# Two more plain chunks in the first FFN, a second VectorE figure in the planner, and one high part at the heads of the second FFNs

## The chip, the cores and the metric

The kernel runs on one core of a Trainium2 chip. The metric is device time in microseconds (us) for one execution, which computes the whole network for one sequence of 256 tokens. A measurement is the median of several executions; beside it stands one execution taken with the hardware profiler, from which all durations of single instructions come.

The engines have short names in the profile: PE is TensorE's matmuls and PEld its weight loads, DVE is VectorE, ACT is ScalarE, POOL is GpSimd, SP issues the DMAs. Each engine works through its own queue in order.

## The reference

Two layers, all in float32, on x of 256 x 1024. The first layer mixes tokens with forgetting attention (FoX), the second with multi-head latent attention (MLA), whose compressed keys and values come from the stream between the layers.

```python
D_MODEL, SEQ, DEPTH, D_FF = 1024, 256, 2, 2816

def post_norm(x, delta, g, b):
    return layer_norm(ALPHA * x + delta, g, b)

def swiglu(x, w_in, w_out):
    h = x @ w_in
    gate, up = h[..., :D_FF], h[..., D_FF:]
    return (jax.nn.silu(gate) * up) @ w_out

for i in range(DEPTH):
    if i == N_A:
        k_nope, k_rope, v_shared = shared_kv(x, kv_w_down, kv_norm, kv_w_up, cos, sin)
    x = post_norm(x, 0.5 * swiglu(x, ffn1_w_in[i], ffn1_w_out[i]), ln_g[i, 0], ln_b[i, 0])
    mix = fox_mixer(...) if i < N_A else mla_mixer(...)
    x = post_norm(x, mix, ln_g[i, 1], ln_b[i, 1])
    x = post_norm(x, 0.5 * swiglu(x, ffn2_w_in[i], ffn2_w_out[i]), ln_g[i, 2], ln_b[i, 2])
    gate = jax.nn.sigmoid(x @ ple_w_gate[i] + ple_b_gate[i])
    x = post_norm(x, gate * (p[i] @ ple_w_proj[i]), ln_g[i, 3], ln_b[i, 3])
```

So there are four FFNs: two per layer, and each has gate and up weights of 1024 x 2816 and output weights of 2816 x 1024.

## The kernel before

**High and low parts.** Every product is made of three matmuls (`mm3`, L581). Each operand is held as a high part (a copy in the type `float32r`, made by ScalarE) and a low part (the operand less its high part, made by VectorE); high x high, high x low and low x high are added up. So each weight passes through ScalarE and VectorE before PE can use it. A *unit* is 128 x 1024 weights at most (`unit_of`, L404); two units share a raw buffer of one megabyte (a group, `group_of`, L387), and of raw buffers there are three. The next group is loaded on SP's queue when the buffer three groups back has been split (`split_done`, L308).

**The planner.** `Stream` (L145) decides, while the program is written, where among the matmuls each unit is split. It keeps clocks of its own for PE, ScalarE, VectorE and the DMAs (`pe_t`, `act_t`, `dve_t`, `dma_t`), which `busy` (L339) advances: a VectorE operation of n columns costs 150 + 1.05 n ns, a ScalarE one 200 + 0.84 n ns, a matmul 0.437 n + 4 ns. A split can be placed in four ways:

- `pump` (L357) is called after most products. It splits one unit if the unit's load should have arrived, a slot is free, and neither ScalarE nor VectorE is more than 1600 ns ahead of PE on these clocks. It does nothing while `hold` is set.
- `ahead` (L192) places only the high part and leaves the low part as `rest`; `later` (L208), or the next split, places the low part. While a `rest` is open, or no slot is free, or the load has not arrived, `ahead` returns without doing anything.
- `fill` (L199) splits up to a given number of units beyond the one in use.
- `use` (L369) splits at once what PE needs now and is not there yet.

There are ten slots `hl0` to `hl9`; others are lent and taken back (`lend`, `reclaim`).

**An FFN** (`ffn`, L697) cuts the 2816 hidden columns into 11 chunks of 256 (`NCH`). For each chunk, gate and up are computed: as `H` (L708), one half of the tokens at a time with x stationary, or as `HT` (L781), transposed, with the weights stationary and 256 tokens moving, 96 matmuls a chunk. The first FFN (`cold`) begins with `first` (L713) for chunk 0, while its weights still arrive, and has only transposed chunks after it; the others begin with H(0, 0), H(1, 0), H(0, 1), H(1, 1), in which the second number is the half of the tokens. In the middle of H(1, 0), after 12 of its matmuls (`HAT`), `other` transposes the other half of x.

The output product is made in one of two ways. *Summed* chunks use a scheme of seven products of blocks in place of eight: `add` (L814) makes sums of the chunk's activations and splits the 896 columns of forms, `Stream.add` (L267) makes sums of the weights (three VectorE operations), four units (`ws`) are split, and `sums` (L833) issues 21 matmuls of 128 x 512 per chunk. *Plain* chunks keep their activations as they are (512 columns, a tile of the ring `g4` of six), split two units (`wout`), and `W` (L904) issues 24 matmuls. The last three chunks (`STAG`) are always plain, and so are those in `early`. The order is: chunks up to 4, `sums` of those of them that are summed, chunks 5 to 7, their `sums`, `combine` (VectorE work that adds the seven products up), chunks 8 to 10, then `W` of the early chunks for both token halves, `W` of chunks 8 to 10 for the first half, the normalization `ln` of that half, `W` for the second half, and its `ln`.

**The mixers** (`fox`, L1089, and `mla`, L1467) run written lists, FOX and ORDER, after (FOX) or from (ORDER) their first projections. In the lists "f n" is `fill`, "a" is `ahead`, "l" is `later`, and "hold 1" and "hold 0" set and clear `hold`. The FOX list sets it from its key and query products on and clears it ahead of the last output products; ORDER begins with "hold 1" and clears it near its end. The per-layer embedding is `ple` (L1022).

`run` (L1786) calls, in order: the first FFN (`cold`), `fox`, the first layer's second FFN, `ple`, the second layer's first FFN (`kv`, which also makes the compressed keys and values), `mla`, the second layer's second FFN, `ple`.

Of the kernel before, what the change touches and what calls it, by code (L numbers as in the profile page):

```python
# [32 lines left out]
SW_H00 = 0  # L33
# [96 lines left out]
class Recorder:  # L130
    def __init__(self):
        self.seq = []
# [12 lines left out]
class Stream:  # L145


    def __init__(self, nc, raw_pool, pool, loads, seq):
        self.nc, self.raw_pool, self.pool, self.loads = nc, raw_pool, pool, loads
        seen = []  # L150
        self.groups = []
        for key in seq:
            g = group_of(key)
            if g not in seen:
                seen.append(g)
                self.groups.append(g)
        members = {g: [] for g in self.groups}
        self.left = {}
        for key in seq:
            if key not in self.left:  # L160
                self.left[key] = 0
                members[group_of(key)].append(key)
            self.left[key] += 1
        self.order = [k for g in self.groups for k in members[g]]
        self.index = {k: i for i, k in enumerate(self.order)}
        self.last_of = {members[g][-1]: i for i, g in enumerate(self.groups)}
        self.raw, self.hl, self.sums, self.added = {}, {}, {}, {}
        self.slots = [f"hl{i}" for i in range(NSLOT)]
        self.slot_of = {}
        self.kept = set()  # L170
        self.loaded = self.ready = 0
        self.done = 0
        self.pending = None
        self.pe_t = self.act_t = self.dve_t = self.dma_t = 0.0
        self.arrives = {}
        self.between = {}
        self.hold = False
        self.rest = None
        self.at = 0
        self.stop = None  # L180

    def load(self, n=NRAW):
        while self.loaded < len(self.groups) and self.loaded < self.done + n:
            g = self.groups[self.loaded]
            r = self.raw_pool.tile([128, 2048], F32, name="raw")
            self.loads(self.nc.sync, g, r, (1, 1, 2, 4)[min(self.loaded, 3)], self.between)
            self.raw[g] = r
            self.dma_t = max(self.dma_t, self.pe_t, self.dve_t) + DMA_NS * WIDTH.get(g[0], 2048) / 2048
            self.arrives[g] = self.dma_t + 2000
            self.loaded += 1  # L190
# [148 lines left out]
    def busy(self, act=0, dve=0, pe=0):  # L339

        if act:
            self.act_t = max(self.act_t, self.pe_t) + 200 + 0.84 * act
        if dve:
            self.dve_t = max(self.dve_t, self.pe_t) + 150 + 1.05 * dve
        if pe:
            self.pe_t += max(109, 0.437 * pe + 4)

# [39 lines left out]
def group_of(key):  # L387
    k = key[0]
    if k in ("win", "wiu", "fv", "kd", "dq"):
        return key[:-1] + (key[-1] // 2,)  # L390
    if k == "ws":
        return key[:-1]
    if k in ("wout", "fvb", "fvc", "fk", "fq", "fo", "pg", "pp", "mo", "qr"):
        return key[:-1] + (key[-1] // 2,)
    if k in ("kvk", "qn"):
        return ("kq", key[-1])
    return key
# [86 lines left out]
class Trunk:  # L484
# [212 lines left out]
    def ffn(self, li, which, lni, kv=False, ple=False, at=None, cold=False, after=()):  # L697


        nc, S = self.nc, self.S  # L700
# [1 line left out]
        g, gT, forms = {}, {}, {}  # L702
        homes = HOMES[:3] if kv else HOMES
        S.reclaim(*homes)
        early = (0,) if cold else (0, 1) if kv else (1,)
        summed = [c for c in range(NCH - STAG) if c not in early]

        def H(c, t, at=None, what=None, sweeps=0):  # L708
            ps = self.bank("h")
            self.moving(ps, t, ("win", li, which, c), 512, at, what, sweeps)  # L710
            act(c, t, ps)

        def first():  # L713

            ps = [self.bank("h") for _ in range(2)]
            key = lambda u: ("win", li, which, 0, u)

            def xs(k):
                def f():
                    self.parts(  # L720
                        self.xT[:, :, 0, k, :], self.xT[:, :, 1, k, :],
                        self.xraw[:, k, :].rearrange("p (t c) -> p t c", c=128),
                    )

                return f

            S.hold = True
            self.spare(self.bank("tr"))
            for u in range(4):
                if u == 0:  # L730
                    head = (("hi", 0, 0, 256), xs(0), ("lo", 0, 0, 256), ("both", 0, 256, 512))
                else:
                    head = (xs(2 * u), ("both", 0, 0, 512))
                S.split_pieces(key(u), head + (xs(2 * u + 1), ("both", 1, 0, 512)))
            for u in range(4):
                w = self.use(key(u))
                for kk in range(2):
                    k = 2 * u + kk
                    for i, j in ((0, 0), (1, 0), (0, 1)):
                        for b in range(4):  # L740
                            self.mm(
                                ps[b // 2][:, 256 * (b % 2) : 256 * (b % 2) + 256],
                                w[:, j, 512 * kk + 128 * b : 512 * kk + 128 * b + 128], self.xT[:, :, i, k, :],
                                (k, i, j, b % 2) == (0, 0, 0, 0), (k, j, b % 2) == (7, 1, 1),
                            )
                if u:
                    S.split()
            S.hold = False
            gt = self.room(0, summed)
            nc.scalar.activation(gt, ps[0], AF.Silu)  # L750
            close(0, gt, ps[1])

        def act(c, t, ps):
            if c not in g:
                g[c] = self.tl([128, 1024], F32, "P", 2) if c == 0 else self.tl([128, 512], F32, "g4", 6)
            gt = g[c][:, 256 * t : 256 * t + 256]
            nc.scalar.activation(gt, ps[:, 0:256], AF.Silu)  # L757
            nc.vector.tensor_tensor(gt, gt, ps[:, 256:512], op=ALU.mult)
            self.S.busy(act=256, dve=256)
# [144 lines left out]
        def W(c, ts, what=None):  # L904
            for kt in range(2):
                w = self.use(("wout", li, which, 2 * c + kt))
                for t in ts:
                    for n in range(2):
                        if kt == 1 and what:
                            what(n)  # L910
                        self.mm3(
                            z[t][n],
                            lambda i: gT[c][:, i, 256 * kt + 128 * t : 256 * kt + 128 * t + 128],
                            lambda i: w[:, i, 512 * n : 512 * n + 512],
                            (t, c, kt) == (0, early[0], 0), (c, kt) == (NCH - 1, 1),
                        )
# [4 lines left out]
        if cold:  # L921
            first()
        else:
            H(0, 0, sweeps=SW_H00)
            S.stop = ("wiu", li, which, 2, 0) if kv else None

            def other():
                self.XT(1)
                S.stop = None

            H(1, 0, HAT, other, SW_H10)
            if kv:
                self.kv_down(1)
            H(0, 1, sweeps=SW_H01)
            H(1, 1)
# [45 lines left out]
        for c in range(n - STAG, n):  # L981
            W(c, (1,), next_x if c == n - 1 else None)
        self.ln(1, z[1], 1.0, 4 * LN_EPS)

    def room(self, c, summed):
        self.full[c] = f = self.tl([128, 1024], F32, "P", 2)
        return f[:, 0:512]
# [912 lines left out]
```

## Time and profile before

| | |
|---|---|
| median of three runs | 1062.66 us |
| the three runs | 1059.51, 1062.89, 1062.66 us |
| the profiled execution, its time | 1060.52 us |
| its span, first to last instruction | 1058.7 us |
| its mean granted TensorE clock | 0.995 |
| HBM read | 200.55 MB, 190 GB/s over the span |

The span falls into these stages, by the first matmul of each (us from the start of the span, rounded): the first FFN from 0, `fox` from 193, the first layer's second FFN from 310, its embedding from 495, the second layer's first FFN from 519, `mla` from 705, the second layer's second FFN from 842, its embedding from 1026.

How to read the lines of the profile: a group or timeline line names the line of the kernel, the engine, the operation, the tiles written and read, shapes (partitions x elements) and count; a bracket in the timeline is the idle time of that engine just before, and what ended it. L589 is the one line by which all matmuls but transposes are issued, L241 and L242 are the high and low part of a weight split, L249 and L253 the same in the form that `ahead` places, L273, L279 and L281 the three weight sums, L803 the product of gate and up, L818, L822 and L823 the activations' sums, L606 a low part of activations. A matmul's tile names tell the stage: `y<-hl,fs` is a product of a split weight with a summed chunk's forms, which lie in `ota`, `otb`, `qk` or `fs`; `h<-xT,hl` is a gate or up product. Matmuls are pipelined, so the time per matmul is the distance from start to start.

### The profile page before, as it was taken

What the parts mean: (1) busy time and instruction counts of PE and PEld (TensorE: products, weight loads), DVE (VectorE), ACT (ScalarE), POOL (GpSimd) and SP (SyncE); (2) the same over time, 40 slices, a digit from 0 to 9 for tenths busy, and PEclk for the clock granted to TensorE, in tenths of its full rate; (3) what the DMA queues carried; (4) which work ended last, traced back from release to release, by engine and by line L of the source; (5) the groups of instructions that cost most, each with busy time, mean ns of one, the idle gap of its engine ahead of it and who ended that gap; (6) DMA issues with size and microseconds to landing.
All of it is one profiled execution on the core that took longest, in us unless ns stands there. A gap on an engine that the chain in (4) does not pass through costs nothing.

```text
span 1058.7 us, 17610 instructions
## 1 busy us (share of the span) xinstructions
PE 1037.5 (98%) x7091; PEld 949.4 (90%) x7091; DVE 883.9 (83%) x1296; ACT 587.0 (55%) x893; POOL 58.3 (6%) x88
## 2 busy tenths in 40 slices
PE   9999899999999999999999999999999999999996
PEld 8979799898878989998889999988999889899986
DVE  5897887868888889977978799778888889899776
ACT  6555465457846464663564646526776474655631
POOL 0000000113400000000040000000000000000000
PEclk9999999999999999999999999999999999999998
DMA  7846367446447465664575646642444465556522
GB/s 280 316 160 217 141 236 252 155 142 225 161 148 264 174 210 199 212 229 168 207 256 182 210 149 229 232 134 105 136 169 151 168 238 200 187 196 224 205 115 80
DMA packets 37477, 202.74 MB, mean 191 GB/s; under 512 B 3970, under 2 KB 9874, under 8 KB 16532
## 3 DMA queue, kind: packets, MB, share of 16 engines
q1 hardware_dynamic: 37396, 201.63, 53.6%
q8 instruction: 55, 0.90, 0.3%
q14 instruction: 26, 0.21, 0.1%
HBM read 200.55 MB, written 1.06 MB: 190 GB/s over the span
## 4 chain that ended last, share of the span: by engine, by line
PE 70%; ACT 2%; DVE 1%; issue 1%; DVEq 0%; ACTq 0%
PE h L589 37%; PE y L589 23%; PE tr L589 8%; PE tr L593 2%; PE h L593 0%; ACT P L1310 0%; ACT hl L241 0%; ACT qk L602 0%; ACT xT L1603 0%; DVE hl L242 0%; DVE x L681 0%; DVE tr L1685 0%; ACT L570 0%; ACT L757 0%; DVE y L1292 0%
## 5 line engine op out<-in xcount | busy, mean ns | idle before, releaser
L589 PE MATMUL h<-xT,hl 128*128 128x256 f32 x3408 | 394.8, 277 | 0.3 <-DVE hl L302 0.3
L589 PEld LDWEIGHTS h<-xT,hl 128*128 128x128 f32 x3408 | 391.8, 188 | 1.4 <-ACT xT L602 0.6
L242 DVE TENSOR_TENSOR hl<-raw,hl 128x1024 fp32r<-128x1024 f32 (+3 forms) x290 | 338.1, 1197 | 49.0 <-ACT hl L241 47.6
L241 ACT ACTIVATE hl<-raw 128x1024 fp32r<-128x1024 f32 (+3 forms) x290 | 287.7, 1031 | 77.3 <-DVE raw L281 21.9
L589 PE MATMUL y<-hl,g 128*128 128x512 f32 x396 | 92.5, 391 | 0.0
L589 PEld LDWEIGHTS y<-hl,g 128*128 128x128 f32 x396 | 73.7, 188 | 14.8
L589 PE MATMUL y<-hl,otb 128*128 128x512 f32 x264 | 69.3, 395 | 0.0
L589 PE MATMUL h<-hl,xT 128*128 128x512 f32 (+2 forms) x306 | 67.1, 371 | 1.4 <-ACT hl L241 1.4
L589 PEld LDWEIGHTS h<-hl,xT 128*128 128x128 f32 x306 | 53.4, 188 | 11.7 <-ACT hl L241 2.5
L589 PEld LDWEIGHTS y<-hl,otb 128*128 128x128 f32 x264 | 48.1, 188 | 9.5 <-DVE otb L606 0.3
L253 DVE TENSOR_TENSOR hl<-raw,hl 128x1024 fp32r<-128x1024 f32 (+2 forms) x42 | 50.0, 1195 | 2.2 <-ACT hl L249 2.1
L589 PE MATMUL y<-hl,ota 128*128 128x512 f32 x192 | 49.9, 393 | 0.0
L673 POOL TENSOR_TENSOR rs<-ve,mhalf 128x1 f32<-128x1 f32 x16 | 15.1, 943 | 623.5 <-DVE ve L672 623.5
L602 ACT ACTIVATE xT<-tr 128x512 fp32r<-128x512 f32 x28 | 16.1, 596 | 58.2 <-PE tr L593 58.2
L242 DVE TENSOR_TENSOR hl<-ts,hl 128x1024 fp32r<-128x1024 f32 (+1 forms) x52 | 48.0, 962 | 0.2 <-ACT hl L241 0.2
L249 ACT ACTIVATE hl<-raw 128x1024 fp32r<-128x1024 f32 (+2 forms) x42 | 43.1, 1029 | 7.1 <-DVE raw L281 6.1
L589 PE MATMUL tr<-xT,hl 128*128 128x256 f32 x384 | 45.3, 277 | 0.0
L589 PEld LDWEIGHTS tr<-xT,hl 128*128 128x128 f32 x384 | 44.5, 188 | 0.4
L589 PE MATMUL y<-hl,xT 128*128 128x512 f32 (+3 forms) x228 | 43.9, 340 | 0.0
L797 ACT ACTIVATE P<-h 128x512 f32<-128x512 f32 x33 | 19.6, 594 | 41.4 <-PE h L589 41.1
L241 ACT ACTIVATE hl<-ts 128x1024 fp32r<-128x1024 f32 (+1 forms) x52 | 41.9, 839 | 0.0
L589 PEld LDWEIGHTS y<-hl,ota 128*128 128x128 f32 x192 | 34.9, 188 | 6.6
(284 smaller groups left out, 1459.3 us busy)
## 6 DMA issues: line engine op xcount, KB each, us to landing
raw<-in_ffn_in_dram SPq DMA_DIRECT2D x85, 1024.0 KB, 4.9
raw<-in_ffn_out_dram SPq DMA_DIRECT2D x44, 1024.0 KB, 5.0
raw<-in_pg_dram SPq DMA_DIRECT2D x8, 1024.0 KB, 5.6
raw<-in_mo_dram SPq DMA_DIRECT2D x8, 1024.0 KB, 4.7
raw<-in_kq_dram SPq DMA_DIRECT2D x8, 640.0 KB, 4.5
gb<-in_ln_g_dram SPq DMA_DIRECT2D x8, 512.0 KB, 6.7
gb<-in_ln_b_dram SPq DMA_DIRECT2D x8, 512.0 KB, 6.3
raw<-in_fk_dram SPq DMA_DIRECT2D x4, 1024.0 KB, 4.9
```

The source lines that it names most:

```text
L241: nc.scalar.activation(hi, src, AF.Copy)
L242: nc.vector.tensor_tensor(lo, src, hi.bitcast(F32), op=ALU.subtract)
L249: nc.scalar.activation(hi, src, AF.Copy)
L253: nc.vector.tensor_tensor(lo, src, hi.bitcast(F32), op=ALU.subtract)
L589: self.nc.tensor.matmul(out, lhsT, rhs, start=start, stop=stop)
L593: self.nc.tensor.transpose(out, in_, self.ident)
L602: self.nc.scalar.activation(hi, src, AF.Copy)
L673: nc.gpsimd.tensor_tensor(rs, ve, self.mhalf, op=ALU.pow)
L797: nc.scalar.activation(gt, ps, AF.Silu)
```

## The change

Three edits, in `Stream` and `ffn`:

1. In the first FFN `early` is (0, 1, 2) where it was (0,). Chunks 1 and 2 become plain: five chunks (3 to 7) are summed where seven were, `sums` of the first group has two chunks where it had four, and `W` of three chunks stands behind chunk 10 where that of one stood. All 11 chunks' gate and up products stay as they are.
2. The constant 150 of a VectorE operation in `busy` becomes `self.fixed`. It is 150 inside an FFN and 80 elsewhere: in both mixers and in the embedding stages.
3. In the second FFN of each layer (neither `cold` nor `kv`), H(0, 0) calls `ahead` once after 12 of its 24 matmuls, as `moving` (L625) does it for `other` in H(1, 0).

```diff
@@ Stream.__init__
         self.stop = None
+        self.fixed = 80
@@ Stream.busy
         if dve:
-            self.dve_t = max(self.dve_t, self.pe_t) + 150 + 1.05 * dve
+            self.dve_t = max(self.dve_t, self.pe_t) + self.fixed + 1.05 * dve
@@ Trunk.ffn
         S.reclaim(*homes)
-        early = (0,) if cold else (0, 1) if kv else (1,)
+        S.fixed = 150
+        early = (0, 1, 2) if cold else (0, 1) if kv else (1,)
         summed = [c for c in range(NCH - STAG) if c not in early]
...
-            H(0, 0, sweeps=SW_H00)
+            H(0, 0, None if kv else 12, S.ahead, SW_H00)
             S.stop = ("wiu", li, which, 2, 0) if kv else None
...
         self.ln(1, z[1], 1.0, 4 * LN_EPS)
+        S.fixed = 80
```

## The prediction

> **What bounds the kernel now.** I read the busy row of the page first, then whom TensorE (PE) waited for (total, times, longest), then the two stretches in which most of it lies.
>
> ```profile
> PE 1037.5 (98%) x7091; PEld 949.4 (90%) x7091; DVE 883.9 (83%) x1296; ACT 587.0 (55%) x893; POOL 58.3 (6%) x88
> ```
>
> ```profile
> PE y L589 <- DVE hl L242: 4.6, 3, 2.1
> PE tr L589 <- DVE hl L242: 1.5, 2, 1.0
> PE h L589 <- ACT hl L241: 1.4, 2, 0.9
> ```
>
> PE is busy for 98% of the span, so a change can win by fewer matmuls or by closing the few holes. Apart from the start, the longest kinds of hole are waits for a weight's low part (VectorE, L242) and for a high part (ScalarE, L241). The first two kinds lie in the first FFN's two `sums` stages, which the first two rows below frame (columns: us; busy time and count of PE, weight loads, VectorE, ScalarE, GpSimd; granted clock; DMA share; GB/s):
>
> ```profile
> 60.68:84.69 24.01, 21.52 (x86) 16.67 (x85) 22.73 (x26) 14.16 (x16) 0.00 (x0) 0.93 0.39 131
> 117.81:137.46 19.65, 15.56 (x65) 11.52 (x64) 18.32 (x23) 10.19 (x12) 0.00 (x0) 1.00 0.42 155
> 419.01:433.30 14.29, 14.29 (x65) 11.82 (x64) 14.08 (x18) 8.33 (x10) 0.00 (x0) 1.00 0.47 154
> ```
>
> ```profile
> 78.39 1.59 PE L589 MATMUL y<-hl,fs 128*128 128x512 f32 x5 [1.89 <-DVE hl L242]
> ...
> 131.42 1.45 PE L589 MATMUL y<-hl,qk 128*128 128x512 f32 x5 [2.12 <-DVE hl L242]
> ```
>
> Each stretch runs from the first product of a `sums` stage to the first matmul of the next chunk: 84 matmuls (four chunks of 21), then 63 (three); the two more in each count are the neighbours at the borders. The third row is the same stage of the first layer's second FFN: 63 matmuls without a hole in 14.29 us, 0.2268 us each. So 84 need 19.05 us, and the first stage loses 24.01 - 19.05 = 4.96 us, the second 19.65 - 14.29 = 5.36 us, together **10.3 us**.
>
> **Why VectorE is late there.** Its timeline around the first stage's start:
>
> ```profile
> 56.05 1.82 DVE L242 TENSOR_TENSOR hl<-ts,hl 128x1024 fp32r<-128x1024 f32 x2
> 57.90 1.23 DVE L273 TENSOR_TENSOR ts<-raw 128x1024 f32<-128x1024 f32 x1
> 59.16 0.69 DVE L279 TENSOR_TENSOR ts<-ts,raw 128x512 f32<-128x512 f32 x1
> 59.89 0.69 DVE L281 TENSOR_TENSOR raw<-ts,raw 128x512 f32<-128x512 f32 x1
> 60.50 1.22 DVE L242 TENSOR_TENSOR hl<-raw,hl 128x1024 fp32r<-128x1024 f32 x1
> 61.63 0.68 DVE L803 TENSOR_TENSOR P<-P,h 128x512 f32<-128x512 f32 x1
> 62.35 0.43 DVE L818 TENSOR_TENSOR P<-P 128x256 f32<-128x256 f32 x1
> 62.81 0.29 DVE L822 TENSOR_TENSOR P<-P 128x128 f32<-128x128 f32 x1
> 63.13 0.29 DVE L823 TENSOR_TENSOR P<-P 128x128 f32<-128x128 f32 x1
> 63.34 1.22 DVE L253 TENSOR_TENSOR hl<-raw,hl 128x1024 fp32r<-128x1024 f32 x1
> 64.48 1.08 DVE L606 TENSOR_TENSOR fs<-P,fs 128x896 fp32r<-128x896 f32 x1
> 65.48 1.82 DVE L242 TENSOR_TENSOR hl<-ts,hl 128x1024 fp32r<-128x1024 f32 x2
> 67.33 1.23 DVE L273 TENSOR_TENSOR ts<-raw 128x1024 f32<-128x1024 f32 x1
> ...
> 82.50 4.63 DVE L242 TENSOR_TENSOR hl<-raw,hl 128x1024 fp32r<-128x1024 f32 x4
> ```
>
> A summed chunk's weights cost three sums (1.23 + 0.69 + 0.69 = 2.61 us) and four lows (1.22 + 1.22 + 1.82 = 4.26 us): 6.87 us, while PE needs 21 x 0.2268 = 4.76 us. VectorE falls back by 2.1 us per chunk and lives on its lead. The rows show how little lead there is: chunk 1's last lows end at 57.87, chunk 2's sums begin at 57.90, and PE starts the products at 60.68.
>
> **Edit 1: chunks 1 and 2 plain.**
> - *PE:* a plain chunk is 24 matmuls of 128x512 (2 row blocks x 2 token halves x 2 column halves x 3 terms), a summed one 21. Two chunks give 6 x 0.2268 = **+1.36 us**, and 48 matmuls come behind the last gate chunk.
> - *VectorE:* per chunk, 6.87 us of weight work becomes two lows (2.44 us), the activations' sums go (0.43 + 0.29 + 0.29 = 1.01 us), and the low of 896 columns shrinks to 512 (1.08 us to about 0.68, the 512-column row at 61.63): 5.84 us, twice that 11.7 us. ScalarE's high parts shrink alike; it is no bound.
> - *DMA:* a chunk's output weights are a megabyte either way, in another order on SP's queue.
> - *First stage after:* 42 matmuls, 60.68 to 70.2. By then VectorE does for chunks 3 and 4 what it now does for 1 and 2: the second chunk's lows end at 61.7, 64.6 and, the last two, 67.3, and chunk 4's own form at 65.56. PE asks for that chunk from 60.68 + 4.76 = 65.44 on, in the order of the lows, for the last two at about 68.2 and 69.5. Nothing is late by more than 0.1 us. **-4.96 us.**
> - *Second stage after:* from 67.33, where VectorE now begins chunk 3's sums, it can make lows of chunk 5 (1.16 us each by the row at 82.50) for 2.9 us before PE asks: a lead of two or three units. Now they begin at 82.50, 2.2 us before PE's 84.69 with no rest of lead. Loads start earlier too, since a raw buffer is refilled only once its weights are split. The second FFN's stage shows that with a lead VectorE just keeps up, 14.08 of 14.29 us busy. I take **-5.36 us**, with bounds 0 and -5.36.
> - *Behind it:* the 48 moved matmuls want 2 x 2.44 us of VectorE in 10.9 us, which only adds lead. The parts of chunks 0, 1, 2, 8, 9, 10 fill the six `g4` tiles exactly; the mixer reuses chunk 0's first, long read by then. No wait is added.
>
> Two further rows concern the clock behind the holes, the first row the loads, the last two the mixers:
>
> ```profile
> 40.00:60.00 20.00, 20.00 (x178) 20.00 (x178) 17.74 (x23) 11.10 (x13) 0.00 (x0) 1.00 0.90 337
> 79.77:83.31 3.54, 3.54 (x10) 2.78 (x9) 3.01 (x4) 3.54 (x5) 0.00 (x0) 0.55 0.75 243
> 131.00:133.00 2.00, 1.58 (x7) 1.29 (x8) 1.59 (x2) 2.00 (x4) 0.00 (x0) 1.00 0.00 0
> 196.00:309.00 113.00, 110.44 (x823) 100.76 (x822) 93.67 (x209) 73.67 (x168) 27.53 (x41) 1.00 0.51 178
> 706.00:841.00 135.00, 134.36 (x860) 120.98 (x859) 114.90 (x263) 86.88 (x206) 3.01 (x4) 1.00 0.44 153
> ```
>
> Behind the 1.89 us hole the granted clock was 0.55 from 79.77 to 83.31, and nine matmuls took 3.54 us in place of 2.04: 1.5 us of the 4.96 are this dip. Behind the 2.12 us hole the clock stayed 1.00, so a hole does not always bring one. I count the dip to the hole, since it follows it directly. The Trainium skill (TensorE: Matmul & The Clock Gate, "What's actually happening") lets the clock fall only after an idle window of about 3.4 us; by that neither hole is long enough and the dip would have another cause and stay, a rival below.
>
> **Edit 2: 80 in place of 150 ns per VectorE operation outside the FFNs.** No instruction is added. The planner charges 80 + 1.05 x 1024 = 1155 ns for a low where it charged 1225; four took 4.63 us, 1158 each, so 80 fits. It lets splits be placed earlier where `pump` is free: the first mixer's head and tail, the second's tail, the embedding stages. Most of both mixers runs under `hold`, where the written lists decide. PE is idle for 2.56 and 0.64 us in them, which bounds the gain at 3.2 us; the loss is bounded by two lows set ahead of a normalization that PE waits for, 2 x 1.22 = 2.4 us. I take **0**, between them, since most of the order stays.
>
> **Edit 3: one high part early at the second FFNs' heads.**
>
> ```profile
> 316.95 2.00 ACT L241 ACTIVATE hl<-raw 128x1024 fp32r<-128x1024 f32 x2
> 317.08 0.42 DVE L758 TENSOR_TENSOR P<-P,h 128x256 f32<-128x256 f32 x1 [0.24 <-ACT P L757]
> 317.42 1.22 DVE L253 TENSOR_TENSOR hl<-raw,hl 128x1024 fp32r<-128x1024 f32 x1
> ...
> 318.05 0.74 PE L589 MATMUL h<-hl,xT 128*128 128x512 f32 x2 [0.92 <-ACT hl L241]
> ...
> 847.82 2.00 ACT L241 ACTIVATE hl<-raw 128x1024 fp32r<-128x1024 f32 x2
> ...
> 848.92 0.50 PE L589 MATMUL h<-hl,xT 128*128 128x512 f32 x1 [0.51 <-ACT hl L241]
> ```
>
> In each head PE waits for a high part that stands in ScalarE's queue behind chunk 0's Silu, which itself waits for PE. In the second layer (848.92) the call moves it into idle time: 0.51 us, of which some goes to the next part or to the normalization, so I take **-0.4** (bounds 0 and -0.5). In the first layer a low deferred by the mixer's list is still open at 317.42 (L253), and `ahead` returns at once while one is open: **0**, unless edit 2 closes it first (-0.9).
>
> **The sum.** -4.96 - 5.36 + 1.36 + 0 - 0.4 = **-9.4 us**. The profiled execution took 1060.52 us, 1.8 more than its span, so 1051.1. The median of the three runs, 1062.66, stands 2.1 us above it, and from that I forecast **1053.3**.
>
> **The rivals.**
> - *The second hole stays.* The lead at chunk 5 is too short and PE catches up as now. For it: VectorE is 99% busy in the hole-free stage too. Against: that stage keeps up. -9.4 + 5.36 = -4.0: 1058.6.
> - *The mixers' new order costs* the 2.4 us at one normalization: -7.0, 1055.7. For it: the lists were written against the old placement. Against: `hold`.
> - *The clock dips anyway:* -9.4 + 1.5 = -7.9, 1054.8. For it: no dip behind the longer hole. Against: the dip begins right behind the other.
> - *Larger gain:* edit 2 closes all 3.2 us of the mixers' holes: -12.6, 1050.1. Against: most of them lie under `hold`.
> - *Slower: the weights do not come.* PE reaches chunk 5 at 70.2 in place of 84.69; if the loads lag, PE waits for them instead of lows, both holes come back, and +1.36 with edit 2's 2.4 leaves +3.8: 1066.5. It decides once a megabyte takes longer than the 5.44 us in which PE uses one, 193 GB/s. Against: 337 GB/s from 40 to 60 us.
> - *An edit that does nothing:* edit 3 in the first layer, counted at 0.
>
> **Chances.** Forecast 0.64, second hole 0.15, mixers lose 0.10, clock 0.05, slower 0.04, larger gain 0.02. What a measurement can tell is 0.3%, 3.2 us, so 1059.5. The second-hole case lies just inside it and counts 0.06 faster, 0.09 same. Faster 0.64 + 0.10 + 0.05 + 0.02 + 0.06 = 0.87, same 0.09, slower 0.04. With the runs' spread (1059.51 to 1062.89) the forecast alone spans 1050 to 1056; with the mixers' loss and the second-hole case the range is 1049.5 to 1059.
>
> **What would show it.** A first `sums` stage of about 9.5 us at clock 1.00; a second of 14.3; VectorE busy some 11 us less; 72 plain-chunk matmuls ahead of chunk 8's; a high part of the half form (L249 here) in the middle of the second layer's H(0, 0). It is wrong if the second stage takes over 17 us, if PE waits for loads after 70 us, or if the mixers' 113 and 135 us grow by over 1 us.

## The result and the profile after

| | before | after |
|---|---|---|
| median, in runs side by side | 1062.78 us | 1054.55 us |
| the runs | 1059.51 to 1064.37 (4) | 1052.94 to 1056.31 (4) |
| ratio, 95% interval | | 0.9927 [0.9898, 0.9955] |
| the profiled execution, its span | 1060.52, 1058.7 us | 1056.31, 1054.5 us |

The changed kernel is 8.2 us faster by the medians; the forecast was 9.4 us, to 1053.3. Measured twice more, it took 1053.3 and 1052.89 us. Its lines stand one or two further down than those of the kernel before (L590 issues the matmuls, L243 and L254 the lows, L242 and L250 the highs).

The page of the changed kernel, busy time by engine:

```profile
PE 1043.3 (99%) x7097; PEld 955.8 (91%) x7097; DVE 872.7 (83%) x1280; ACT 584.5 (55%) x889; POOL 57.5 (5%) x88
```

The changed kernel's waits of PE (total, times, longest):

```profile
PE y L566 <- POOL mhalf L551: 1.2, 1, 1.2
PE h L590 <- DVE PT L607: 0.7, 2, 0.5
PE h L590 <- ACT p L603: 0.5, 1, 0.5
PE h L590 <- DVE otb L607: 0.2, 1, 0.2
PE h L590 <- DVE hl L303: 0.2, 1, 0.2
```

VectorE has 11.2 us less to do (883.9 to 872.7; about 11 were forecast), and every wait for the low or high part of a weight is gone but one of 0.2 us. The two `sums` stages of the changed kernel, framed as before:

```profile
63.87:73.51 9.64, 9.64 (x44) 7.90 (x43) 9.54 (x13) 7.86 (x10) 0.00 (x0) 1.00 0.31 110
107.87:122.50 14.63, 14.63 (x66) 11.77 (x64) 14.35 (x19) 9.46 (x13) 0.00 (x0) 1.00 0.37 128
```

42 matmuls in 9.64 us and 63 in 14.63, without a hole and at full clock. Around the first of them VectorE does what the working said (the last two lows of the second chunk at 67.3, here at 69.85), 2.5 us later, while PE gets there 3.2 us later in this execution:

```profile
68.03 1.82 DVE L243 TENSOR_TENSOR hl<-ts,hl 128x1024 fp32r<-128x1024 f32 x2
69.77 1.22 DVE L243 TENSOR_TENSOR hl<-raw,hl 128x1024 fp32r<-128x1024 f32 x1
70.94 0.69 DVE L860 SCALAR_TENSOR_TENSOR x<-x,h 128x512 f32<-128x512 f32 x1
71.54 5.76 DVE L243 TENSOR_TENSOR hl<-raw,hl 128x1024 fp32r<-128x1024 f32 x5
```

From 71.54 on it makes five lows of chunk 5 in a row, the lead that chunk 5 lacked.

### The profile page after: what moved, and what is told of

Read it like the earlier page. It is cut to its first block, busy times and chain, and to the rows that moved or that the text cites. A ratio compares the mean times of both kernels' runs of the same rounds, so it can differ in the third digit from the quotient of the medians.

```text
span 1054.5 us, 17598 instructions
## 1 busy us (share of the span) xinstructions
PE 1043.3 (99%) x7097; PEld 955.8 (91%) x7097; DVE 872.7 (83%) x1280; ACT 584.5 (55%) x889; POOL 57.5 (5%) x88
## 3 DMA queue, kind: packets, MB, share of 16 engines
HBM read 200.55 MB, written 1.06 MB: 191 GB/s over the span
## 4 chain that ended last, share of the span: by engine, by line
PE 71%; DVE 2%; ACT 1%; issue 0%; DVEq 0%; ACTq 0%
PE h L590 37%; PE y L590 23%; PE tr L590 8%; PE tr L594 2%; PE h L594 0%; DVE hl L243 0%; DVE x L682 0%; DVE tr L1688 0%; ACT qk L603 0%; ACT P L1313 0%; DVE h L1295 0%; DVE y L1295 0%; DVE hl L254 0%; ACT xT L1606 0%; DVE PT L607 0%
## 5 line engine op out<-in xcount | busy, mean ns | idle before, releaser
L590 PE MATMUL h<-xT,hl 128*128 128x256 f32 x3384 | 397.0, 279 | 0.2 <-DVE hl L303 0.2
L590 PEld LDWEIGHTS h<-xT,hl 128*128 128x128 f32 x3384 | 393.4, 189 | 1.9 <-ACT xT L603 0.6
L243 DVE TENSOR_TENSOR hl<-raw,hl 128x1024 fp32r<-128x1024 f32 (+3 forms) x289 | 336.3, 1195 | 52.5 <-ACT hl L242 51.1
L242 ACT ACTIVATE hl<-raw 128x1024 fp32r<-128x1024 f32 (+3 forms) x289 | 286.3, 1030 | 75.6 <-PE y L590 31.8
L590 PE MATMUL y<-hl,g 128*128 128x512 f32 x432 | 100.3, 390 | 0.0
L590 PEld LDWEIGHTS y<-hl,g 128*128 128x128 f32 x432 | 80.6, 188 | 16.3
L590 PE MATMUL y<-hl,otb 128*128 128x512 f32 x264 | 70.2, 398 | 0.0
L590 PE MATMUL h<-hl,xT 128*128 128x512 f32 (+2 forms) x300 | 65.2, 370 | 0.0
L590 PEld LDWEIGHTS h<-hl,xT 128*128 128x128 f32 x300 | 52.5, 188 | 9.3
L590 PEld LDWEIGHTS y<-hl,otb 128*128 128x128 f32 x264 | 48.2, 188 | 10.3 <-DVE otb L607 0.3
L254 DVE TENSOR_TENSOR hl<-raw,hl 128x1024 fp32r<-128x1024 f32 (+2 forms) x42 | 50.2, 1199 | 1.5 <-ACT hl L250 1.4
L590 PE MATMUL y<-hl,ota 128*128 128x512 f32 x192 | 49.9, 394 | 0.0
L590 PE MATMUL y<-hl,xT 128*128 128x512 f32 (+3 forms) x258 | 47.8, 333 | 0.0
L250 ACT ACTIVATE hl<-raw 128x1024 fp32r<-128x1024 f32 (+2 forms) x42 | 43.1, 1029 | 6.8 <-DVE raw L282 5.6
L590 PE MATMUL tr<-xT,hl 128*128 128x256 f32 x384 | 45.6, 278 | 0.0
L590 PEld LDWEIGHTS tr<-xT,hl 128*128 128x128 f32 x384 | 44.9, 188 | 0.3
L243 DVE TENSOR_TENSOR hl<-ts,hl 128x1024 fp32r<-128x1024 f32 (+1 forms) x47 | 43.4, 958 | 2.0 <-ACT hl L242 2.0
L590 PEld LDWEIGHTS y<-hl,xT 128*128 128x128 f32 x258 | 39.8, 188 | 4.5 <-ACT xT L603 0.4
L590 PEld LDWEIGHTS y<-hl,ota 128*128 128x128 f32 x192 | 35.0, 188 | 6.6
```

Source lines behind the costliest of these rows:

```text
L242: nc.scalar.activation(hi, src, AF.Copy)
L243: nc.vector.tensor_tensor(lo, src, hi.bitcast(F32), op=ALU.subtract)
L250: nc.scalar.activation(hi, src, AF.Copy)
L254: nc.vector.tensor_tensor(lo, src, hi.bitcast(F32), op=ALU.subtract)
L590: self.nc.tensor.matmul(out, lhsT, rhs, start=start, stop=stop)
```

## The experiments

All stage times below run from the first transposes of one stage's x to those of the next, in the profiled execution (us). The last column is the embedding of the second layer to the end.

| | FFN 1 | fox | FFN 2 | emb. | FFN 3 | mla | FFN 4 | emb. |
|---|---|---|---|---|---|---|---|---|
| before | 191.00 | 116.37 | 184.92 | 23.19 | 187.61 | 136.49 | 184.52 | 34.64 |
| edit 1 alone (e1) | 183.02 | 114.78 | 185.43 | 23.36 | 188.16 | 137.23 | 185.05 | 34.72 |
| edit 2 alone (e2) | 189.14 | 115.57 | 183.83 | 23.19 | 187.61 | 136.62 | 185.78 | 34.20 |
| edit 3 alone (e3) | 191.05 | 116.51 | 184.91 | 23.19 | 187.61 | 136.50 | 184.63 | 34.66 |
| all three, first profile | 186.98 | 115.46 | 184.24 | 23.36 | 188.16 | 137.19 | 184.40 | 34.73 |
| all three again (e4) | 183.07 | 114.96 | 184.26 | 23.35 | 188.17 | 137.22 | 184.39 | 34.72 |
| all three, third time (e7) | 184.23 | 115.59 | 184.23 | 23.36 | 188.16 | 137.26 | 184.39 | 34.72 |
| all three, old places (e5) | 184.73 | 114.66 | 183.85 | 23.19 | 187.61 | 136.48 | 183.89 | 34.23 |
| before, new places (e6) | 189.36 | 116.53 | 185.44 | 23.35 | 188.17 | 137.25 | 185.06 | 35.13 |

The last six columns repeat within 0.1 us for one program, so tenths can be read there. The first two do not: between three profiles of the same program FFN 1 moved by 3.9 us, and fox by 0.6 us with the same waits of PE.

### e1 to e4: one edit at a time, and all three again

```diff
 e1   early = (0, 1, 2) if cold else (0, 1) if kv else (1,)
 e2   self.fixed: 80, and 150 from S.reclaim to the last ln of an FFN
 e3   H(0, 0, None if kv else 12, S.ahead, SW_H00)
```

> Edit 1 alone (early = (0, 1, 2) in the first FFN, 150 ns everywhere, no early high part). If the gain is VectorE's lead in the first FFN, this kernel has nearly all of it: 7 to 9 us less than before, both sums stages without a hole (about 9.6 and 14.3 us), and the two head holes (0.9 and 0.5 us) as before. If the gain is the planner's new figure, this kernel gains under 2 us.

> Edit 2 alone (80 ns outside the FFNs). By the forecast within 1.5 us of before, with both holes of the first FFN in place (stages of about 24 and 19.6 us); the hole at the first layer's second FFN head (0.9 us) may go, since edit 2 can close the open low part. If edit 2 carries the gain, 5 us or more less than before. Both holes give a second look at the clock: a dip behind the first one again, if the hole brings it.

> Edit 3 alone. By the forecast 0.4 us less than before, which times can't tell; in the profile the hole at the second layer's second FFN head (0.5 us) goes and the one at the first layer's (0.9 us) stays, since a low part is still open there and the call returns. If the call works in both heads, both go. The first FFN's holes stay.

> The changed kernel once more, unchanged. 1052 to 1057 us. In its first profile matmuls of 256 columns stood 118 ns apart in long stretches (10 to 63 us and 73 to 109 us) where before they stood 113 ns apart, 4% slower at a granted clock of 1.00. If that belongs to the execution, the stretches lie elsewhere this time and the first sums stage begins at about 60.7 us in place of 63.9; if it belongs to the program, they lie at the same places.

| | median us | ratio to before |
|---|---|---|
| e1 | 1054.07 | 0.9931 [0.9917, 0.9945] |
| e2 | 1060.55 | 0.9986 [0.9974, 0.9997] |
| e3 | 1062.52 | 1.0007 [0.9998, 1.0016] |
| e4 | 1053.3 | 0.9921 [0.9906, 0.9936] |

Edit 1 is the change: its first `sums` stage took 9.65 us (24.01 before), its second 14.84 (19.65), and the two holes at the heads stayed. e2 moved the time by no more than was expected, and e3 not beyond its interval. In e2 the hole at the head of FFN 2 went; in e3 it stayed, and the one at the head of FFN 4 gave way to a wait of 0.4 us for a low part. In e4 the first stage began at 60.96 us, where the first profile of this program had 63.87, so the slow pace ahead of it belongs to the execution. Three things in the table had not been forecast.

**Fox gains with edit 1 alone.** It took 1.59 us less; the kernel before has one hole of 1.03 us in it, which goes (timeline, all from one stretch):

```profile
240.35 1.05 ACT L241 ACTIVATE hl<-raw 128x1024 fp32r<-128x1024 f32 x1
...
241.29 1.05 ACT L249 ACTIVATE hl<-raw 128x1024 fp32r<-128x1024 f32 x1
...
242.25 0.85 ACT L602 ACTIVATE PT<-tr 128x512 fp32r<-128x512 f32 x2
...
242.98 0.80 ACT L1329 ACTIVATE P<-P,su 128x128 f32<-128x128 f32 x2
...
243.50 1.59 PE L589 MATMUL h<-PT,g 128*128 128x512 f32 x6 [1.03 <-ACT P L1329]
```

The same step with edit 1 alone:

```profile
232.09 0.86 ACT L602 ACTIVATE PT<-tr 128x512 fp32r<-128x512 f32 x2
...
232.82 0.81 ACT L1329 ACTIVATE P<-P,su 128x128 f32<-128x128 f32 x2
...
234.05 1.21 PE L589 MATMUL h<-PT,g 128*128 128x512 f32 x6
```

Before, two high parts of weights stand in ScalarE's queue ahead of the high part of PT, for which PE's next product waits. The list places them there by number. With edit 1 the mixer starts one unit further along than before, and by the step ahead of this one it is two units further; those weights are split already, and the list finds less to place. From the `P` of the step ahead to the `P` of this one ScalarE makes four high parts of weights in the kernel before, in e3, e6 and e8 (the last two below), and all four have this hole; it makes two in e1, e2, e10 and the changed kernel, and none of them has it. A fixed list is no fixed order: how much it issues depends on what came before.

**Edit 2 alone moves the wait at the head of FFN 4 and makes it longer.** Edit 2 alone, at that head:

```profile
848.21 2.95 ACT L242 ACTIVATE hl<-raw 128x1024 fp32r<-128x1024 f32 x3
...
849.31 1.88 PE L590 MATMUL h<-hl,xT 128*128 128x512 f32 x7 [1.63 <-ACT hl L242]
```

1.63 us in place of 0.51; with edit 3 as well it is gone. In the changed kernel the high part that `ahead` places stands within H(0, 0), which begins at 837.66, and the products run through:

```profile
838.61 1.05 ACT L250 ACTIVATE hl<-raw 128x1024 fp32r<-128x1024 f32 x1
...
840.44 5.67 PE L590 MATMUL h<-hl,xT 128*128 128x512 f32 x24
```

**Edit 1 costs time where nothing waits:** FFN 2 +0.5, its embedding +0.17, FFN 3 +0.55, mla +0.74, FFN 4 +0.53, in e1 and in all three together alike. In FFN 3 PE is busy from end to end in both kernels, so the matmuls themselves are slower. e5 and e6 are about this.

### e5, e6, e7: the places of five tiles

A tile of the on-chip memory gets its address when its name is first used. In the kernel before, chunk 1's forms (`ota`) come ahead of the first weight sums (`ts`); with chunks 1 and 2 plain it is the other way round, and `ota`, `otb`, `ts`, `qk` and `gb` lie elsewhere, in the whole program. e5 takes the names in the old order in the changed kernel; e6 takes them in the new order in the kernel before. All engines' instructions and their order stay the same.

```diff
 e5, ahead of the first weight sum
+for t in ("ota", "otb", "ts", "qk"): self.pool.tile(...)
 e6, ahead of the first ota
+for t in ("ts", "ota", "gap0", "gb", "gap1"): self.tl(...)
```

> The changed kernel with the same instructions in the same order on every engine; only five tiles of the on-chip memory (ota, otb, qk, gb, ts) lie where they lie in the kernel before. Edit 1 moves them, since a tile gets its place when its name is first used and ts is now used ahead of ota. Theory P (the places set the pace of the matmuls): the stages that edit 1 slowed without a hole come back: the first layer's second FFN from 184.3 to 183.8 us, its embedding from 23.36 to 23.19, the second layer's first FFN from 188.16 to 187.6, mla from 137.2 to 136.5, together 1.9 us; the first FFN stays at about 183. What fox does tells whether its gain of 1.5 us with edit 1 is of the places too: 116.3 if so, and then the whole gains only 0.4 us; 114.9 if not, and then the whole falls from about 1053.3 to about 1051.4 us. Rival O (the order of the splits and the slots of the weights set it): every stage as in the changed kernel within 0.1 us.

> The kernel before with the same instructions in the same order; only the five tiles lie where edit 1 puts them. Theory P: the second layer's first FFN 188.16 us in place of 187.61, mla 137.2 in place of 136.5, the first layer's second FFN and embedding 185.4 and 23.36 in place of 184.92 and 23.19: slower by 1.9 us, or by 0.4 if fox falls from 116.4 to 114.9 with them. Rival O: every stage as in the kernel before within 0.1 us.

> The changed kernel again, beside the last two on the same chip: ratio 0.992 to 0.993. Its stages: fox about 115, the second layer's first FFN 188.16, mla 137.2. The pace of 118 ns per 256-column matmul over 10 to 63 us, seen in one of two executions so far, comes back or not; if it comes with the execution, the first FFN takes 187 or 183 us.

Theory P holds, to 0.1 us in each of the four stages behind fox that it named, and rival O falls (FFN 1, at 184.73 in place of about 183, lies within its spread); FFN 4 and the last embedding, which it had not named, move by 0.5 us each as well. FFN 3 and mla, kernel before:

```profile
515.48:703.09 187.61, 187.61 (x1292) 173.64 (x1291) 154.61 (x186) 100.18 (x123) 14.76 (x20) 1.00 0.57 200
703.09:839.58 136.49, 135.85 (x867) 122.34 (x866) 116.83 (x265) 88.13 (x207) 3.01 (x4) 1.00 0.44 151
```

e6, the same program with the new places:

```profile
514.68:702.85 188.17, 188.17 (x1292) 173.69 (x1291) 154.55 (x186) 100.20 (x123) 13.76 (x20) 1.00 0.57 200
702.85:840.10 137.25, 136.68 (x868) 122.75 (x867) 116.92 (x265) 88.17 (x207) 3.00 (x4) 1.00 0.43 151
```

e5, the changed kernel with the old places:

```profile
506.43:694.04 187.61, 187.61 (x1292) 173.65 (x1290) 154.62 (x186) 100.23 (x123) 14.76 (x20) 1.00 0.57 200
694.04:830.52 136.48, 135.84 (x868) 122.33 (x867) 116.86 (x264) 89.12 (x208) 3.01 (x4) 1.00 0.44 151
```

The same matmuls at the same clock take 0.56 and 0.76 us longer or shorter by the addresses alone. From e7 to e5 the stages behind fox lose 2.87 us in all (0.38, 0.17, 0.55, 0.78, 0.50, 0.49). Fox does not come back to 116.4, so its gain is of the splits.

e5 took **1050.38 us** (1049.97 to 1050.6), ratio 0.9887 [0.9874, 0.9901], faster than both kernels; e7 beside it 1052.89 us (1052.23 to 1053.72), 0.9909 [0.9894, 0.9924]. e6 is less clear: 1062.48 us, 1.0006 [0.9996, 1.0017], where its stages behind FFN 1 add up to 3.2 us. Its profile has FFN 1 shorter by 1.64 us, with no dip of the clock behind the first hole; how often the timed runs have that dip was not seen, so for e6 the stages carry the finding and the time does not.

### e8: VectorE's work taken away

The kernel before; the third weight sum is not issued for the first FFN.

```diff
-        else:
+        elif g[1:3] != (0, "ffn1"):
             tt(r[:, 0:512], self.sums[g][:, 1024:1536], r[:, 1536:2048], op=ALU.add)
```

> The kernel before with the third weight sum (0.69 us of VectorE) left out for the seven summed chunks of the first FFN: that part of the weights' sums is not computed, and nothing else is moved. Theory V (the two holes are VectorE's backlog on the summed chunks' weights): VectorE has 4 x 0.69 us less to do ahead of the first stage's last products and 3 x 0.69 us more ahead of the second's; the first hole of 1.89 us and most of the small ones go, the first stage falls from 24.0 to 19 to 20.5 us with no dip, the second from 19.65 to 15.5 to 17.6 us. Rival L (the weights' loads or the high parts of ScalarE hold the low parts up): both stages stay within 0.5 us of 24.0 (22.4 without the dip) and 19.65.

19.71 and 16.54 us, both inside what theory V gave and outside the rival's. Loads and high parts are as they were, so the holes are VectorE's backlog. (One run, 1055.98 us.)

### e9: VectorE's work added

The changed kernel; the first weight sum is issued twice.

```diff
             tt(s[:, 0:1024]..., r[:, 512:1536]..., op=ALU.add)
+            if g[1:3] == (0, "ffn1"):
+                tt(s[:, 0:1024]..., r[:, 512:1536]..., op=ALU.add)
```

> The changed kernel with the first weight sum (1.23 us of VectorE) issued twice for each of the five summed chunks of the first FFN; the same values are written again, and nothing else is moved. It measures how much room VectorE has left where the holes were. If the first stage has no room, as the forecast's rows have it (nothing late by more than 0.1 us), the two extra sums before its last products cost 1.2 to 2.5 us there: 10.9 to 12.1 us in place of 9.65. The second stage has the lead of five lows made at 69 to 75 us; three extra sums are 3.7 us: 14.6 us if the lead covers them, 18.3 if it covers nothing. If VectorE were not what bounds these stages, both stay at 9.65 and 14.6 to 14.8.

11.33 us in the first stage, inside what was expected without room, but not all of the added work: of 2 x 1.23 = 2.46 us 1.68 came out, most of it as waits for chunk 4's own forms (0.74 and 0.42 us). The second took 19.72, above the 18.3 allowed for a lead that covers nothing. Timeline of e9:

```profile
120.30 2.22 PE L595 MATMUL y<-hl,qk 128*128 128x512 f32 x5 [3.34 <-DVE hl L243]
122.31 1.49 PE L595 MATMUL h<-hl,qk 128*128 128x512 f32 x3
...
125.22 0.86 PE L595 MATMUL y<-hl,qk 128*128 128x512 f32 x3
```

Of 3 x 1.23 = 3.69 us added, 3.34 come out as one hole, so the changed kernel's second stage has next to no room. Behind the hole three matmuls take 1.49 us in place of 0.86: a dip of the clock adds the rest, which the expectation had left out. The single run took 1060.25 us: 6 us of extra VectorE work (5 x 1.23), with this dip, undo most of the change.

### e10: half of edit 1

```diff
-        early = (0,) if cold else (0, 1) if kv else (1,)
+        early = (0, 1) if cold else (0, 1) if kv else (1,)
```

> The kernel before with only chunk 1 made plain beside chunk 0: half of edit 1, no other edit. Theory V: VectorE falls back 2.1 us per summed chunk, so the first stage's holes without the dip (22.4 less 19.05 us = 3.3) shrink to about 1.2: 63 matmuls of 0.2268 us and that, 15.5 us; the second stage starts with more lead and takes 14.8 to 17.5 us. Fewer lows by a fixed size would give 17.6 us (14.29 + 3.3) in the first and 19.6 in the second if the holes do not come from the backlog. The five tiles lie in a third way here (otb, qk, gb and ts moved, ota not), so the stages behind the mixer may take times other than those of the kernel before (187.61 and 136.5 us) and of the changed one (188.16 and 137.2); if they do, with the same instructions, that speaks for the places again.

1057.43 us, 0.9965 [0.9951, 0.9979]. The first stage took 15.50 us, just what a backlog of 2.1 us per summed chunk gives. The second took 19.56, more than the 17.5 expected:

```profile
122.15 1.67 PE L589 MATMUL y<-hl,qk 128*128 128x512 f32 x5 [1.89 <-DVE hl L242]
123.61 1.48 PE L589 MATMUL h<-hl,qk 128*128 128x512 f32 x3
```

The hole is a little shorter than before (1.89, 2.12), and again a dip follows it, which the second hole of the kernel before did not have. The lead of one plain chunk more is not enough for chunks 5 to 7; that of two is, with next to nothing to spare.

In e10 the five tiles lie in a third way, and this tells which of them matters. Addresses are those of the compiled program, in bytes from the start of a partition, modulo 256: the ten slots of split weights are at 224 in all three kernels. The same `sums` stage of FFN 3, kernel before (`otb` at 224, `qk` at 224):

```profile
588.28 0.84 PE L589 MATMUL h<-hl,otb 128*128 128x512 f32 x3
588.96 0.84 PE L589 MATMUL y<-hl,otb 128*128 128x512 f32 x3
...
593.04 0.84 PE L589 MATMUL h<-hl,qk 128*128 128x512 f32 x3
593.72 0.84 PE L589 MATMUL y<-hl,qk 128*128 128x512 f32 x3
```

e6, the changed kernel's places (`otb` at 96, `qk` at 96):

```profile
587.60 0.87 PE L593 MATMUL h<-hl,otb 128*128 128x512 f32 x3
588.30 0.85 PE L593 MATMUL y<-hl,otb 128*128 128x512 f32 x3
...
592.48 0.87 PE L593 MATMUL h<-hl,qk 128*128 128x512 f32 x3
593.18 0.85 PE L593 MATMUL y<-hl,qk 128*128 128x512 f32 x3
```

e10 (`otb` at 224, `qk` at 96):

```profile
584.09 0.84 PE L589 MATMUL h<-hl,otb 128*128 128x512 f32 x3
584.76 0.84 PE L589 MATMUL y<-hl,otb 128*128 128x512 f32 x3
...
588.88 0.87 PE L589 MATMUL h<-hl,qk 128*128 128x512 f32 x3
589.59 0.85 PE L589 MATMUL y<-hl,qk 128*128 128x512 f32 x3
```

From start to start three matmuls take 0.68 us at 224 and 0.70 at 96, tile by tile. `ota` moved as well, but to an address with the same rest (224), and its pace is the same everywhere; so did `otb` in e10. The 21 products of a chunk take 0.12 us longer with their tile at 96. FFN 3 has four such groups, two with `otb` and two with `qk`, which gives 0.48 of its 0.56 us. In e10, with `qk` alone at 96, FFN 3 took 187.89 us, half of the way, and mla 137.02.

### e11 and e12: edits 3 and 2 in company, old places

```diff
 e11 (e5 without edit 3)   H(0, 0, sweeps=SW_H00)
 e12 (e5 without edit 2)   self.dve_t = max(self.dve_t, self.pe_t) + 150 + 1.05 * dve
```

> Edits 1 and 2 without edit 3, with the five tiles at the places they have in the kernel before. Theory I (edits 2 and 3 belong together): edit 2 alone moved the wait at the head of the second layer's second FFN instead of closing it, 1.63 us in place of 0.51, and edit 3 closes it; so this FFN takes 185.8 us in place of 183.9 and the whole about 1.9 us more than with edit 3, 1052.3 in place of 1050.4. Rival: edit 3 is worth what it was worth alone, within 0.1 us: 183.9, and 1050.4. The stages ahead of it are the same in both: fox 114.7, the first layer's second FFN 183.85, the second layer's first FFN 187.61, mla 136.5.

> Edits 1 and 3 without edit 2, with the five tiles at their places in the kernel before. If edit 2's share is what it removes at the heads and in the last embedding: fox 114.8 (edit 1 alone closes its hole), the first layer's second FFN 184.9 with its hole of 0.92 us back (183.85 with edit 2), the second layer's second FFN 184.6 (183.9), its embedding 34.65 (34.2), so 2.2 us more than with all three: about 1052.6. If edit 2 is worth only what it showed alone in the whole time (1.5 us, of which 0.8 lay in fox, where edit 1 now does the same): 1051.1.

e11: FFN 4 took 185.78 us, and the whole 1052.42 (1049.9 to 1053.59; ratio 0.9912 [0.9899, 0.9926]): beside edit 2, edit 3 is worth 1.9 us in its stage, and the theory of the pair holds; the times' intervals touch. Its one wait at that head is back:

```profile
PE h L593 <- ACT hl L242: 1.6, 1, 1.6
```

e12: FFN 2 took 184.91 us with its hole of 0.92 back, as expected. But FFN 4 took 184.36 (184.6 expected), the last embedding 34.24 (34.65) and fox 114.26, below e5. So with edits 1 and 3 beside it edit 2 is worth 1.06 and 0.47 us at the two heads and 0.15 in mla. Fox took 0.40 us less without it, which lies within the 0.6 us by which fox differs between profiles of one program. The last embedding is as short without edit 2 as with it; why was not found. The whole took 1051.16 us (1049.39 to 1052.26; 0.9901 [0.9887, 0.9914]), nearer to the lower of the two expected, 1051.1; against e5 no difference is resolved.

## Why the prediction came out as it did

The time was near and the main mechanism right. That it came so near is in part luck: the sum left out three terms of over 1 us (fox, the head of FFN 2, the places of tiles), and they nearly cancel. From the profile of the kernel before to that of e4 (its chunks 5 to 7 have the same pace as before):

| step | forecast | measured |
|---|---|---|
| first hole | -4.96 | 24.01 - 9.66 less the 42 moved matmuls at 0.2268: -4.82 |
| second hole | -5.36 | 19.65 - 14.83: -4.82 |
| six more matmuls | +1.36 | +1.43, with the pace (below) |
| edit 2, fox's hole | 0 | -1.41 (edit 1 alone: -1.59; the other two profiles of the changed kernel: -0.91, -0.78) |
| edit 2, FFN 2's head | 0 | -1.17 (e4 less e1) |
| edit 3, FFN 4's head | -0.4 | -0.66 (e4 less e1), with edit 2 |
| places of tiles (e1 less before, FFN 2 to FFN 4) | not seen | +0.51 + 0.17 + 0.55 + 0.74 + 0.53 = +2.5 |
| start of the first stage, last embedding | 0 | +0.28, +0.08 |
| sum | -9.4 | -8.6 |

- *Both holes* were closed for the reason given; e8, e9 and e10 bear it out by taking VectorE's work away, adding it and halving the edit. The statement that nothing would be late by more than 0.1 us was right for the first stage, and nearly tight: of 2.46 us of sums added there 1.68 came out. The second stage keeps 0.54 us above 14.29 in e4: 0.24 by the places of `otb` and `qk`, and nearly all of the rest at the first products of its third chunk. At the old places it keeps 0.52 (e5): 0.32 at one wait for a low part, also at the third chunk, and 0.20 in the matmuls behind it, whose slower pace was not explained. So the lead forecast for this stage is just short of enough.
- *The clock's dip* was counted to the hole. That was right for the profile it was read from, but the dip does not come each time: with the very same 1.89 us hole e3 has it and e2 has not. The first stage takes 24.0 us with it and 22.4 without, so 1.6 of the 4.96 us hung on the execution. What decides is where the hole falls on a grid of 3.41 us (worked out in the last section). In e3 the whole hole lies in one step of the grid, and the clock (third figure from the right) is 0.50 in the next:

```profile
75.64:79.05 3.41, 1.52 (x7) 0.97 (x6) 3.27 (x5) 1.61 (x2) 0.00 (x0) 1.00 0.37 154
79.05:82.46 3.41, 3.41 (x9) 2.63 (x8) 2.40 (x3) 3.41 (x5) 0.00 (x0) 0.50 0.45 132
```

In e2 a border of the grid cuts it, and PE is busy for 1.89 and 3.06 us of the two steps; the clock stays:

```profile
74.42:77.83 3.41, 1.89 (x9) 1.23 (x7) 3.34 (x4) 0.71 (x1) 0.00 (x0) 1.00 0.62 262
77.83:81.25 3.42, 3.06 (x13) 2.55 (x14) 3.35 (x5) 3.42 (x5) 0.00 (x0) 1.00 0.26 46
```

- *The step that failed is the choice of 0 for edit 2*, with its reason that most of the order stays under `hold`. `hold` stops `pump`, but the lists' own `fill` and `ahead` issue only what is not split yet, so a lead won ahead of them leaves them less to place. e2 gains 0.8 us in fox, 1.1 in FFN 2 and 0.4 in the last embedding, and loses 1.3 in FFN 4 and 0.1 in mla; with the other two edits the loss in FFN 4 goes (e12). Of the rivals, the mixers' loss did not come, and of the larger gain's 3.2 us fox gave 1.4, which edit 1 alone gives too.
- *Edit 3* was priced alone, at -0.4. Alone it gives nothing (e3: 184.63 against 184.52; the wait comes back as one for a low). Its worth lies in edit 2's company (e11). The clause "unless edit 2 closes it first (-0.9)" gave the right size for the first layer by another way: FFN 2's hole closes with edit 2 alone, without the call of edit 3, and e3 alone leaves it.
- *Slower, since the weights do not come*, and *the second hole stays* did not happen. e10 shows how near the second was: with one chunk fewer the hole stays.
- *Not in the sum at all:* the places of five tiles, 2.87 us behind fox by e7 and e5. The prediction asked whether the mixers' stages would grow by over 1 us, and mla grew by 0.7, but the cause was none of its rivals.

## What to carry to other kernels

A stage whose side engine needs more time per chunk than the main engine (6.87 against 4.76 us here) lives on its lead; count the lead at the stage's start, and expect a cheaper form of a few chunks to pay twice, in the stage and in the next one's lead. An edit that changes when a buffer is first used can move addresses in the whole program: compare the address map before reading tenths in stages that the edit does not touch. Small edits at a stage's head are priced together, since the next late item is often the other edit's.

## What the runs showed of the hardware

- **Matmul pace depends on addresses.** With split weights in slots at 224 modulo 256, products with `otb` or `qk` at 96 run at 0.70 us for three, at 224 at 0.68 us, at a granted clock of 1.00 in both. The Trainium skill (TensorE: Matmul & The Clock Gate, "Step-by-step: what each phase is for") says that loading the next weights takes no read bandwidth from the running matmul. Here the pace hangs on where the two operands lie; whether the two bear on each other no run here shows. That the rest modulo 256 is the rule is read from three placements of two tiles and was not tried further.
- **The pace of FFN 1 belongs to the execution.** One program took 186.98, 183.07 and 184.23 us there. Chunks 5 to 7, from the first `sums` stage's end to the second's start, took 34.36 us in the first profile of the changed kernel, in e7 and in e8, and 33.1 in the other eleven profiles of this study, at full clock and with PE busy throughout. No value between the two was seen. Why stays open.
- **Whether a short hole halves the clock hangs on where it falls.** In every profile here the granted clock changes on a grid of 3.413 us: from its first rise to 1.00 to each later change the time is a whole number of such steps (the kernel before: 71.68 us or 21 steps, then one, then 284), and each dip behind a hole is one step at 0.50. Up to the end of PE's work the clock fell behind the steps in which PE was idle for 1.89 us (the kernel before, e3, e10) and 3.05 us (e9), and behind none with 1.56 us or less. The 2.12 us hole of the kernel before is cut by a border into 1.44 and 0.68, and the clock stayed at 1.00. So the limit lies between 1.56 and 1.89 us idle of one step. The Trainium skill (same page, "What's actually happening") has a window of about 3.4 us that runs free of the program, and the grid agrees; it gives a whole idle window as the condition for the fall, and here 1.89 us of one were enough.
